# Joined borders with the squares from three sums, 18 idle products at the start, and a new order of the expert weights

## The chip, the cores and the metric

The kernel runs on one core of a Trainium2 chip. The metric is the device time of one execution in microseconds (us). The core's engines are TensorE (PE in the rows; PEld is its loading of weights), VectorE (DVE), ScalarE (ACT), GpSimd (POOL) and SyncE (SP), whose queue issues nearly all the transfers (DMA). Each engine runs its own queue in order; waits between the engines go by semaphores.

## The reference

Two layers of a decoder trunk on 256 tokens of width 1024. Each sub-layer normalises x, scales and shifts it by values made from c (adaLN), computes a token mixer or a channel mixer, and adds the normalised result times a gate:

```python
for layer in range(DEPTH):
    mod = (c_act @ w_ada[layer] + b_ada[layer])[:, None, :]
    shift_m, scale_m, gate_m, shift_f, scale_f, gate_f = jnp.split(mod, 6, axis=-1)
    h = rms_norm(x, g_pre_mix[layer]) * (1.0 + scale_m) + shift_m
    m = hybrid_mixer(h, w_in[layer], w_out[layer], ...)
    x = x + gate_m * rms_norm(m, g_post_mix[layer])
    h = rms_norm(x, g_pre_ffn[layer]) * (1.0 + scale_f) + shift_f
    if layer % 2 == 0:
        f = swiglu(h, ffn_w_gate[i], ffn_w_up[i], ffn_w_down[i])
    else:
        f = moe_swiglu(h, moe_w_router[i], moe_b_router[i], moe_w_gate[i], moe_w_up[i], moe_w_down[i])
    x = x + gate_f * rms_norm(f, g_post_ffn[layer])
```

The mixer joins 8 stick-breaking heads and 8 sparse heads. The channel mixer of layer 0 is one SwiGLU of width 2816; that of layer 1 sends each token to 2 of 8 experts, each a SwiGLU of width 3584. All is float32.

## The kernel before

**Stages.** Layer 0's mixer, layer 0's dense channel mixer (`ffn`), layer 1's mixer, the router, then the experts one after the other (`moe`). Tokens lie in two tiles t of 128. From 587 us to 1423 us of the span the experts run.

**Weights.** All weights come in units of 1 MB (`U`, 128x2048 float32). Units are loaded into a ring of six buffers named `raw` (`load`, L165 to L168), in `moe` also into tiles named `unit` (whole units with the tag a8, L994; half units with the tags g, y, f, t4, L1002). SP's queue issues these loads in the order of the program, and each waits there until its buffer is free. A place in the `moe` stage's memory is free when the mixer's tiles that lay there have been read for the last time. The list `plan` in `stream` says into which buffers the first 18 units of the experts go; later units take `raw`, t4 and a8 in turn (`ring`).

**Products.** A product in float32 is taken apart: ACT rounds a half unit to `whi` (L180), DVE (for the first units after a border GpSimd, by `lead`) subtracts it into `wlo` (L181), and PE makes three products (`mm3`, L196 to L198). An expert with few tokens ("short") is multiplied in plain float32 instead, with the weights as the moving side (L1054). An expert has 42 units: of each of its 7 chunks two for `moe_gate`, two for `moe_up`, two for `moe_down`, where a chunk's `moe_down` stands in the stream behind the next chunk's gate. The second gate unit of the second expert is therefore the 42nd of the stream.

**Borders.** Between layer 0's mixer and `ffn` (border 1) and between `ffn` and layer 1's mixer (border 2) stands, for each tile: `update` (L400: the squares of the result m by ACT, mg = m times the gate row by DVE, x += mg * r by DVE), `measure` (L240: the squares of the new x by ACT), `rows` (L248: xn = x * r' by DVE, L256), and `norm_parts` (L296): 8 transposes `xnT` on PE (L308), scale and shift `hf` by DVE and ACT in turn (L312, L314), `hh` by ACT (L316), `hlo` by DVE (L317). The first product of the next stage needs both. In border 1 m is itself a sum of two projected halves (L545), which starts when the sum of squares `sss` (L774) is there.

**Router.** `scorer` (L851) transposes the raw x (`xT`) and makes the logits with 8 columns; `route` (L880) picks experts and places; `gather` (L1152) brings the tokens of the first expert together by products with a 0/1 matrix.

**Start.** `first` (L330) transposes the normalised x (8 products `xnT`, L267) and waits for scale and shift of the first projection, which come from the adaLN weights; `pb` is the product for the bias table.

**Order.** The rows of each engine's queue stand in the order in which the program calls them, moved only where `behind` asks for one instruction to follow another.

## Time and profile before

| | us |
|---|---|
| time, median of 3 runs (lowest, highest) | 1440.67 (1439.38, 1440.95) |
| the profiled execution | 1441.2 |
| its span | 1439.4 |
| PE busy, share of the span | 1366.9, 95% |
| DVE busy | 984.6, 68% |
| ACT busy | 769.4, 53% |
| POOL busy | 16.6, 1% |

The mean clock that TensorE was granted is 0.971 of full speed. The span is cut by stage in the windows of the rows below, and read as follows: a stage in which PE is always busy is bound by PE; where PE sits idle, the timeline names what ended the idle time; a stage in which the DMA moves its top rate all along has transfers as its limit or close to it.

### The profile page before, as it was taken

How to read it: one execution, taken by the hardware profiler on the slowest of the kernel's cores; microseconds unless marked ns; L12 is line 12 of the kernel's file. 1: busy time of each engine (PE TensorE's matmuls, PEld its weight loads, DVE VectorE, ACT ScalarE, POOL GpSimd, SP SyncE). 2: the span in 40 equal slices, each digit the busy share in tenths (PEclk: the TensorE clock that was granted, in tenths of full speed). 3: DMA queues.
4: the chain of work that ended last, by engine and by line, in shares of the span. 5: the costliest groups of instructions: out<-in, count | busy, mean ns of one | idle time of the engine just before them, and what ended most of it. 6: DMA issues, size and time to landing. Idle time of an engine off the chain costs nothing.

```text
span 1439.4 us, 20261 instructions
## 1 busy us (share of the span) xinstructions
PE 1366.9 (95%) x7408; PEld 974.5 (68%) x7408; DVE 984.6 (68%) x1578; ACT 769.4 (53%) x1179; POOL 16.6 (1%) x24
## 2 busy tenths in 40 slices
PE   5899969999979999999999999999999999999996
PEld 5767659999877687534787434887435888788432
DVE  7677988877565785424998425997416989999413
ACT  3463654444554556223777324786325877787322
POOL 0100010000100000000000000000000000000000
PEclk9989979999989999899999999999999999999998
DMA  9935929888435285999999999999999999999994
GB/s 370 341 130 189 342 94 350 322 318 331 161 123 203 91 319 176 393 400 426 426 426 426 400 413 426 426 426 426 396 425 426 427 425 378 338 371 372 375 426 179
DMA packets 73479, 482.52 MB, mean 335 GB/s; under 512 B 10315, under 2 KB 10484, under 8 KB 18588
## 3 DMA queue, kind: packets, MB, share of 16 engines
q1 hardware_dynamic: 72876, 479.91, 83.5%
q0 software_dynamic: 496, 1.25, 0.4%
q8 instruction: 60, 0.98, 0.3%
q14 instruction: 47, 0.39, 0.1%
HBM read 479.87 MB, written 1.25 MB: 334 GB/s over the span
## 4 chain that ended last, share of the span: by engine, by line
PE 65%; DVE 3%; ACT 1%; issue 1%; DVEq 0%; ACTq 0%
PE moe_gate L1054 7%; PE moe_up L1054 7%; PE yacc L1054 7%; PE moe_gate L197 4%; PE moe_gate L196 4%; PE moe_gate L198 4%; PE yacc L197 4%; PE yacc L198 3%; PE yacc L196 3%; PE moe_up L197 3%; PE moe_up L198 3%; PE moe_up L196 3%; PE gT L1112 2%; PE gather L1190 1%; PE po L628 1%; DVE wlo L181 1%
## 5 line engine op out<-in xcount | busy, mean ns | idle before, releaser
L180 ACT ACTIVATE whi<-raw 128x1024 fp32r<-128x1024 f32 x260 | 271.7, 1058 | 156.4 <-PE ffn_gate L197 30.2
L181 DVE TENSOR_TENSOR wlo<-raw,whi 128x1024 fp32r<-128x1024 f32 x256 | 306.9, 1222 | 69.5 <-ACT whi L180 62.2
L181 DVE TENSOR_TENSOR wlo<-unit,whi 128x1024 fp32r<-128x1024 f32 x202 | 236.6, 1220 | 9.6 <-ACT whi L180 5.4
L180 ACT ACTIVATE whi<-unit 128x1024 fp32r<-128x1024 f32 x202 | 208.3, 1057 | 34.0 <-PE moe_up L198 17.0
L208 DVE CUSTOM_DVE_ANT_0 raw<-raw,cb,sm 128x1024 f32<-128x1024 f32 x96 | 120.5, 1278 | 1.0 <-DMA raw<-in_w_ada_dram 1.0
L1102 DVE TENSOR_TENSOR sg<-moe_gate,sg 64x512 f32<-64x512 f32 x28 | 19.1, 681 | 113.4 <-ACT sg L1101 113.4
L197 PE MATMUL moe_up<-wlo,xgh 128*128 128x512 f32 x224 | 88.5, 395 | 3.9 <-DVE wlo L181 3.9
L197 PE MATMUL yacc<-wlo,g 128*128 128x512 f32 x224 | 89.5, 400 | 0.3 <-DVE wlo L181 0.3
L196 PE MATMUL moe_gate<-whi,xgh 128*128 128x512 f32 x224 | 88.3, 394 | 0.0
L197 PE MATMUL moe_gate<-wlo,xgh 128*128 128x512 f32 x224 | 87.9, 392 | 0.0
L196 PE MATMUL moe_up<-whi,xgh 128*128 128x512 f32 x224 | 87.8, 392 | 0.0
L196 PE MATMUL yacc<-whi,g 128*128 128x512 f32 x224 | 87.8, 392 | 0.0
L198 PE MATMUL yacc<-whi,g 128*128 128x512 f32 x224 | 87.5, 391 | 0.0
L198 PE MATMUL moe_gate<-whi,xgl 128*128 128x512 f32 x224 | 87.4, 390 | 0.0
L198 PE MATMUL moe_up<-whi,xgl 128*128 128x512 f32 x224 | 87.4, 390 | 0.0
L1102 DVE TENSOR_TENSOR up<-moe_up,up 64x512 f32<-64x512 f32 x28 | 19.1, 683 | 72.7 <-ACT up L1101 72.7
L1054 PE MATMUL moe_up<-unit,xf 128*64 128x512 f32 x288 | 66.3, 596 | 0.0
L1054 PE MATMUL yacc<-unit,gf 128*64 128x512 f32 x272 | 62.2, 593 | 0.0
L1054 PE MATMUL moe_gate<-unit,xf 128*64 128x512 f32 x240 | 57.1, 598 | 0.0
L1101 ACT ACTIVATE sg<-moe_gate 64x512 f32<-64x512 f32 x28 | 16.6, 594 | 72.6 <-PE moe_gate L1054 72.5
L197 PEld LDWEIGHTS moe_up<-wlo,xgh 128*128 128x128 f32 x224 | 42.1, 188 | 16.5 <-DVE wlo L181 8.2
L196 PE MATMUL ffn_gate<-hh,whi 128*128 128x256 f32 x176 | 50.5, 287 | 2.5 <-ACT hh L316 2.4
(415 smaller groups left out, 2900.2 us busy)
## 6 DMA issues: line engine op xcount, KB each, us to landing
unit<-in_moe_gate_dram SPq DMA_DIRECT2D x66, 1024.0 KB, 12.9
unit<-in_moe_up_dram SPq DMA_DIRECT2D x56, 1024.0 KB, 12.5
unit<-in_moe_down_dram SPq DMA_DIRECT2D x54, 1024.0 KB, 14.6
raw<-in_w_ada_dram SPq DMA_DIRECT2D x48, 1024.0 KB, 6.8
raw<-in_moe_gate_dram SPq DMA_DIRECT2D x46, 1024.0 KB, 13.5
raw<-in_moe_down_dram SPq DMA_DIRECT2D x45, 1024.0 KB, 14.0
raw<-in_moe_up_dram SPq DMA_DIRECT2D x44, 1024.0 KB, 13.3
raw<-in_w_in_dram SPq DMA_DIRECT2D x16, 1024.0 KB, 6.2
```

Of the source, the lines that this page charges most:

```text
L180: self.last_hi = nc.scalar.activation(hi, w, AF.Copy)
L181: last_lo = (nc.gpsimd if self.count < 2 else nc.vector).tensor_sub(lo, w, hi.bitcast(F32))
L196: nc.tensor.matmul(out, lhsT=ahi, rhs=bhi, start=first, stop=False, skip_group_check=True)
L197: nc.tensor.matmul(out, lhsT=ahi, rhs=blo, start=False, stop=False, skip_group_check=True)
L198: nc.tensor.matmul(out, lhsT=alo, rhs=bhi, start=False, stop=last, skip_group_check=True)
L208: self.nc.vector.tensor_tensor_reduce(w[:, j], w[:, j], self.cb, 1.0, self.sm[:, b:b + 1], OP.mult, OP.add, self.modc[:, l, o:o + 1])
L628: nc.tensor.matmul(po[64 * g:64 * g + 64, :], lhsT=lhs, rhs=rhs, start=first[g], stop=last, skip_group_check=True)
L1054: m = nc.tensor.matmul(out[64 * kk:64 * kk + 64], lhsT=x[:, k], rhs=w[:, 512 * kk:512 * kk + 512], start=first and h == 0, stop=last and h ...
L1101: nc.scalar.activation(to, p[64:128], AF.Copy)
L1102: nc.vector.tensor_add(to, p[0:64], to)
L1112: nc.tensor.transpose(tr[0][:, j, 0:n], sg[0:n, P * j:P * j + P], self.ident[0:n, 0:n])
L1190: nc.tensor.matmul(p[:, a], lhsT=self.x[:, t, P * k:P * k + P], rhs=both[:, t], start=a == 0 and t == 0, stop=t == 1, skip_group_check=True)
```

## The change

**Borders.** `update`, `rows` and the transposes at both borders go. `ahead` prepares, before the result m is there: a row `ssr` of scale and gain laid over all partitions (8 more transposes on PE, named `rows`), `xsr` = x * ssr for both tiles (4 operations on 512 columns), the old sum of squares `sum0`, ssr times the gate row (2 operations), and the shift as `shT` (one transpose). `join` takes the squares of the new x from three sums: of x*x (known), of mg*x (`tensor_tensor_reduce`, 2 per tile), and of mg*mg (ACT). xs = m*ssr*gate*r + xsr is formed on DVE; the transposition is a product of xs with a diagonal matrix `dg` of r' (16 float32 products), added in PSUM to a product that lays down the shift (4 products of 512 columns, which need only `shT`). `hh` and `hlo` are taken from PSUM directly.

**Weights at the borders.** `foretell` loads and converts the first unit of the next stage before the border; GpSimd converts nothing any more. The conversions of `w_gates` wait for the border's last instructions.

**Idle products.** Products in bfloat16 on a matrix of ones, 512 columns wide, whose result nobody reads: 18 at the start between `xnT` and `pb`, 6, 4 and 7 in the scorer, 2 in the router.

**Router.** The logits have the weights as the stationary side (four groups of 32 columns, added up by one more product). The gather of a short expert has 128 columns where it had 64.

**Expert stream.** The new `plan` begins with whole units in the places a7 and a3, then the six `raw`, then the others. Every load follows the one before it from the first unit on.

```diff
-                            self.ffn(l, Phase(ph, t4=3, t2=3, h8=2))
+                            self.ffn(l, Phase(ph, t4=4, t2=4, h8=3))
...
-                self.moe(L - 1, Phase(ph, t4=2, t2=3, x4=2, f=2, y=2, g=2, a8=8))
+                self.moe(L - 1, Phase(ph, t4=2, t2=3, x4=2, f=2, y=2, g=2, **{f"a{i}": 1 for i in range(8)}))
...
+        if self.fore:
+            parts, self.fore = self.fore, None
+            yield from parts
+            return
...
-            with self.behind(*(self.chain if 2 <= self.count < 4 else self.lead if self.count < 2 else ())):
+            with self.behind(*(self.chain if self.count < 2 else ())):
                 self.last_hi = nc.scalar.activation(hi, w, AF.Copy)
-                last_lo = (nc.gpsimd if self.count < 2 else nc.vector).tensor_sub(lo, w, hi.bitcast(F32))
...
+    def foretell(self, src):
...
+        nc, parts, after = self.nc, [], self.conv
+        raw = self.load(src)
+        for h in range(2):
+            w = raw[:, h * (U // 2):(h + 1) * (U // 2)]
+            hi, lo = (self.mix.tile([P, U // 2], F32R, name=n, bufs=2) for n in ("fhi", "flo"))
+            with self.behind(*after):
+                nc.scalar.activation(hi, w, AF.Copy)
+                nc.vector.tensor_sub(lo, w, hi.bitcast(F32))
+            parts.append((h, *(p.rearrange("p (k f) -> p k f", k=4) for p in (hi, lo))))
+        return parts
...
+    def ahead(self, ph, l, gain, scale_i, shift_i, gm):
...
+        row = self.mix.tile([P, D], F32, name="ssr")
+        self.rows_of(self.affine(l, gain, scale_i), row)
+        p = self.bank("t", "shT")
+        nc.tensor.transpose(p[0:KT, 0:P], self.mod(l, shift_i), self.ident)
+        self.shT = self.mix.tile([KT, P], F32, name="shT")
+        nc.scalar.activation(self.shT, p[0:KT, 0:P], AF.Copy)
+        self.xsr = ph.tile([P, 2 * D + LINE], F32, name="xsr", tag="h8")[:, 0:2 * D].rearrange("p (t c) -> p t c", t=2)
+        self.sum0 = self.small.tile([P, 2], F32, name="sum0")
+        for t in range(2):
+            q = self.xsq[t]
+            nc.vector.tensor_add(self.sum0[:, t:t + 1], q[:, 0:1], q[:, 1:2])
+            for i in range(2):
+                cs = slice(512 * i, 512 * i + 512)
+                nc.vector.tensor_mul(self.xsr[:, t, cs], self.x[:, t, cs], row[:, cs])
+        for i in range(2):
+            cs = slice(512 * i, 512 * i + 512)
+            nc.vector.tensor_mul(row[:, cs], row[:, cs], gm[:, cs])
+        self.both_rows, self.pieces = (gm, row), []
+
+    def join(self, ph, t, src):
...
+        nc = self.nc
+        gm, gms = self.both_rows
+        ssq = self.small.tile([P, 2], F32, name="ssu")
+        sj = self.small.tile([P, 8], F32, name="sj")
+        mg = ph.tile([P, D], F32, name="mg", tag="t4")
+        mgs = src(None)
+        if mgs is None:
+            mgs = ph.tile([P, D], F32, name="mgs", tag="t4")
+        half = [slice(0, 512), slice(512, 1024)]
+        for i, cs in enumerate(half):
+            piece = src(i)
+            scr = self.small.tile([P, 512], BF16, name="scr")
+            nc.scalar.activation(scr, piece, AF.Square, accum_out=ssq[:, i:i + 1])
+            nc.vector.tensor_mul(mg[:, cs], piece, gm[:, cs])
+            scr = self.small.tile([P, 512], BF16, name="scr")
+            nc.scalar.activation(scr, mg[:, cs], AF.Square, accum_out=sj[:, i:i + 1])
+            junk = ph.tile([P, 512], F32, name="junk", tag="t2")
+            nc.vector.tensor_tensor_reduce(junk, mg[:, cs], self.x[:, t, cs], 2.0, sj[:, 2:3] if i else 0.0, OP.mult, OP.add,
+                                           sj[:, 2 + i:3 + i])
+            nc.vector.tensor_mul(mgs[:, cs], piece, gms[:, cs])
+        r = self.rstd(ssq[:, 1:2], D, "ru", base=ssq[:, 0:1])
+        nc.vector.tensor_add(sj[:, 4:5], sj[:, 0:1], sj[:, 1:2])
+        nc.vector.scalar_tensor_tensor(sj[:, 5:6], sj[:, 4:5], r, sj[:, 3:4], op0=OP.mult, op1=OP.add)
+        nc.vector.scalar_tensor_tensor(sj[:, 6:7], sj[:, 5:6], r, self.sum0[:, t:t + 1], op0=OP.mult, op1=OP.add)
+        nc.vector.tensor_scalar(sj[:, 7:8], sj[:, 6:7], 0.0, None, op0=OP.max)
+        r2 = self.rstd(sj[:, 7:8], D, "rn")
+        for i, cs in enumerate(half):
+            nc.vector.scalar_tensor_tensor(mgs[:, cs], mgs[:, cs], r, self.xsr[:, t, cs], op0=OP.mult, op1=OP.add)
+        dg = ph.tile([P, P], F32, name="dg", tag="t2")
+        scaled = nc.vector.tensor_scalar(dg, self.ident, r2, None, op0=OP.mult).ins
+        self.pieces.append((mgs, dg))
+        for cs in half:
+            with self.behind(*([scaled] if t else [])):
+                nc.vector.scalar_tensor_tensor(self.x[:, t, cs], mg[:, cs], r, self.x[:, t, cs], op0=OP.mult, op1=OP.add)
+        if t == 0:
+            return
+        self.hT = [[self.bank(b, "hT").rearrange("p (k t) -> p k t", k=4) for h in range(2)] for b in "sp"]
+        for out, (xs, dg) in zip(self.hT, self.pieces):
+            for h, p in enumerate(out):
+                nc.tensor.matmul(p, lhsT=self.shT, rhs=self.ident[0:KT, 4 * h:4 * h + 4, None].to_broadcast([KT, 4, P]),
+                                 start=True, stop=False, skip_group_check=True)
+            for h, p in enumerate(out):
+                for i in range(4):
+                    k = 4 * h + i
+                    nc.tensor.matmul(p[:, i], lhsT=xs[:, P * k:P * k + P], rhs=dg, start=False, stop=True, skip_group_check=True)
...
             if q == 0:
+                self.idle(18, self.last_turn, banks[5].rearrange("p m t -> p (m t)"))
...
             r = self.rstd(sq, 512, "ro")
...
+            if l == 0 and j == 0:
+                self.fore = self.foretell(self.ins["ffn_gate"][0])
...
             if l == 0:
-                self.update(ph, t, piece, gm, nc.vector)
+                self.join(ph, t, piece)
...
+        if l == 0:
+            self.ahead(ph, 0, G_PRE_FFN, 4, 3, gm)
...
+                self.fore = self.foretell(self.ins["w_in"][11 - 6])
...
+            if u == 7:
+                self.ahead(ph, 1, G_PRE_MIX, 1, 0, gm)
...
-            self.update(ph, t, lambda n: None if n is None else acc[t][n], gm, nc.vector)
+            self.join(ph, t, lambda n: None if n is None else acc[t][n])
...
+    def idle(self, n, after, warm=None):
...
+        warm = self.bank("p", "warm") if warm is None else warm
+        with self.behind(after):
+            for i in range(n):
+                self.nc.tensor.matmul(warm.rearrange("p (a t) -> p a t", a=4), lhsT=self.one,
+                                      rhs=self.one[:, None].to_broadcast([P, 4, P]), start=True, stop=True)
...
+        ws = ph.tile([P, KT, 32], F32, name="ws", tag="t2")
+        nc.gpsimd.memset(ws, 0.0)
...
+            if t:
+                self.total(after)
...
+                if h:
+                    self.idle(6 - 2 * t, last.ins)
...
-                    k = 4 * h + i
-                    nc.tensor.matmul(pl[:, 0:E], lhsT=xT[:, i], rhs=ws[:, k], start=k == 0, stop=k == KT - 1)
+                    nc.tensor.matmul(pl[32 * i:32 * i + 32, 0:P], lhsT=ws[:, 4 * h + i], rhs=xT[:, i], start=h == 0, stop=h == 1,
...
+                return nc.tensor.matmul(pl[:, 2 * P:2 * P + E], lhsT=part, rhs=self.sel[:, 0:E], start=True, stop=True,
...
+                self.idle(7, total(after).ins)
...
+        self.idle(2, last.ins)
...
-            plan = [None, None, None, "g", None, None, None, "y", "f", "t4", "a8", "a8", "a8", "a8", "a8", "a8", "a8", "a8"]
-            ring = [t for t in plan if t in (None, "t4", "a8")]
+            plan = ["a7", "a3", None, None, None, None, None, None, "g", "y", "a2", "a4", "a1", "a5", "a0", "a6", "f", "t4"]
+            ring = [t for t in plan if t not in ("g", "y", "f")]
...
-        ahead = [next(fetch) for i in range(4)]
+        made["g"] = tiles("g")
...
-        ahead += [next(fetch) for i in range(14)]
-        made.clear()
+        for i in range(8):
+            made[f"a{i}"] = ph.tile([P, U], F32, name="unit", tag=f"a{i}")
+        ahead = [next(fetch) for i in range(18)]
```

SP's queue, from the last load of layer 1's mixer (`in_w_out_dram`) to the experts' first loads. `raw` is the ring of six, `unit` a tile in the memory of `moe`. Before:

```order
L168 DMA raw<-in_w_out_dram 128x2048 [waits DVE_49]
L168 DMA raw<-in_moe_gate_dram 128x2048 [waits DMAHW5_49,DVE_49]
L168 DMA raw<-in_moe_gate_dram 128x2048 [waits DVE_49]
L168 DMA raw<-in_moe_up_dram 128x2048 [waits DMAHW6_49,DVE_49]
L168 DMA raw<-in_moe_gate_dram 128x2048 [waits DMAHW7_49,DVE_49]
L168 DMA raw<-in_moe_gate_dram 128x2048 [waits DMAHW0_49,DVE_49]
L168 DMA raw<-in_moe_up_dram 128x2048 [waits DMAHW1_49,DVE_49]
L1002 DMA unit<-in_moe_up_dram 128x1024 [waits PE_49]
```

After:

```order
L168 DMA raw<-in_w_out_dram 128x2048 [waits DVE_49]
L1112 DMA unit<-in_moe_gate_dram 128x2048 [waits DVE_49,PE_49,Activation_49]
L1112 DMA unit<-in_moe_gate_dram 128x2048 [waits DVE_49,PE_49,Pool_49]
L168 DMA raw<-in_moe_up_dram 128x2048 [waits DMAHW5_49]
L168 DMA raw<-in_moe_up_dram 128x2048
L168 DMA raw<-in_moe_gate_dram 128x2048 [waits DMAHW6_49]
L168 DMA raw<-in_moe_gate_dram 128x2048 [waits DMAHW7_49]
L168 DMA raw<-in_moe_up_dram 128x2048 [waits DMAHW0_49]
```

Two loads into the memory of `moe` now stand ahead of the six into `raw`. The waits of the first (a7) are for tiles of layer 1's mixer, on DVE for the second tile's last addition to x; those of the second (a3) are for `ws`, which lay there and is read last by the last product of the logits, and for the copy `xT`.

DVE's queue at border 1, from `sss` on. Before, up to the first tile's addition to x:

```order
L774 COPY sss<-ssb 128x2
L293 SCALAR_TENSOR_TENSOR ss<-modc,sm 128x8
L227 TENSOR_SCALAR rov<-sss,halfeps 128x2
L231 SCALAR_TENSOR_TENSOR rov<-ror,rov 128x1 x2
L232 SCALAR_TENSOR_TENSOR ror<-rov,ror 128x2
L545 SCALAR_TENSOR_TENSOR m<-wo,ror,m 128x512
L412 TENSOR_TENSOR m<-m,gm 128x512
...
L418 SCALAR_TENSOR_TENSOR x<-m,rur,x 128x512 x2
```

After, up to the same tile's three sums (`junk,sj` is the sum of mg*x):

```order
L863 COPY sss<-ssb 128x2
L331 TENSOR_TENSOR xsr<-x,ssr 128x512 x4
L334 TENSOR_TENSOR ssr<-ssr,gm 128x512 x2
L244 TENSOR_SCALAR rov<-sss,halfeps 128x2
L199 TENSOR_TENSOR flo<-raw,fhi 128x1024
L248 SCALAR_TENSOR_TENSOR rov<-ror,rov 128x1 x2
L249 SCALAR_TENSOR_TENSOR ror<-rov,ror 128x2
L632 SCALAR_TENSOR_TENSOR m<-wo,ror,m 128x512 x2
L354 TENSOR_TENSOR mg<-m,gm 128x512 x2
L358 ISA junk,sj<-mg,x 128x512
L358 ISA sj 128x1
L360 TENSOR_TENSOR m<-m,ssr 128x512
```

Between `sss` and the first sum for m stand seven more large operations (four `xsr`, two `ssr`, one `flo`); each half of m is then read by three DVE operations (L354, L358, L360) where one (L412) read it.

## Rows read from the trace of the kernel before

**Rows 1.** The page: TensorE's and the other engines' busy time over the whole span, and the shares of the chain of work that ended last.

```profile
PE 1366.9 (95%) x7408; PEld 974.5 (68%) x7408; DVE 984.6 (68%) x1578; ACT 769.4 (53%) x1179; POOL 16.6 (1%) x24
...
PE 65%; DVE 3%; ACT 1%; issue 1%; DVEq 0%; ACTq 0%
```

**Rows 2.** Windows of the expert stage: stretch in us, its length, busy time of PE, PEld, DVE, ACT and POOL, the granted clock as a share of full speed, the DMA share, GB/s.

```profile
575.00:640.00 65.00, 62.31 (x295) 29.84 (x297) 25.38 (x90) 18.19 (x36) 0.00 (x0) 0.89 0.94 389
640.00:700.00 60.00, 58.37 (x266) 30.62 (x263) 31.81 (x35) 27.93 (x37) 0.00 (x0) 1.00 1.01 426
...
820.00:880.00 60.00, 60.00 (x285) 22.23 (x284) 18.75 (x35) 19.41 (x34) 0.00 (x0) 1.00 0.99 407
```

**Rows 3.** Timeline of SP's queue between 518 and 600 us (start, time taken to issue, what, count), and last, of the experts' gate weights in 515 to 700 us, the time from issue to landing (minimum, median, maximum).

```profile
524.29 2.67 SPq L168 DMA_DIRECT2D raw<-in_moe_gate_dram  x2
...
548.03 0.33 SPq L168 DMA_DIRECT2D raw<-in_moe_up_dram  x1
555.19 1.91 SPq L1002 DMA_DIRECT2D unit<-in_moe_up_dram  x4
576.90 0.80 SPq L994 DMA_DIRECT2D unit<-in_moe_gate_dram  x2
...
DMA to landing us min/median/max: 4.8/13.6/19.9
```

**Rows 4.** The first expert: the timeline's first row of its products on PE, then two rows of the chain of waits (start, length; the gate products of two chunks that follow each other), and the timeline's row of ACT with the conversion of the second expert's first two units.

```profile
586.89 3.45 PE L1054 MATMUL moe_gate<-raw,xf 128*64 128x512 f32 x10
...
646.96 3.58 PE moe_gate L1054 x16
...
657.79 3.58 PE moe_gate L1054 x16
...
665.36 3.89 ACT L180 ACTIVATE whi<-unit 128x1024 fp32r<-128x1024 f32 x4
```

**Rows 5.** Timeline of PE at border 1 (in brackets the idle time before, and what ended it).

```profile
189.26 0.39 PE L198 MATMUL wo<-whi,os 128*128 128x512 f32 x1
198.44 4.02 PE L308 MATMUL xnT<-ident,xn 128*128 128x128 f32 x16 [8.79 <-DVE xn L256]
204.82 0.58 PE L196 MATMUL ffn_gate<-hh,whi 128*128 128x256 f32 x1 [2.36 <-ACT hh L316]
```

**Rows 6.** Timeline of DVE at border 1, and in the last row of POOL.

```profile
180.30 0.16 DVE L774 COPY sss<-ssb 128x2 f32<-128x2 f32 x1 [0.35 <-PE ssb L772]
...
187.03 2.06 DVE L231 SCALAR_TENSOR_TENSOR ruv<-rur,ruv 128x1 f32<-128x1 f32 x1 [0.55 <-ACT rur L228]
189.13 2.27 DVE L232 SCALAR_TENSOR_TENSOR rur<-ruv,rur 128x1 f32<-128x1 f32 x1
191.44 1.42 DVE L418 SCALAR_TENSOR_TENSOR x<-m,rur,x 128x512 f32<-128x512 f32 x2
192.77 0.75 DVE L545 SCALAR_TENSOR_TENSOR m<-wo,ror,m 128x512 f32<-128x512 f32 x1
...
199.95 0.88 DVE L256 TENSOR_SCALAR xn<-x,rnr 128x512 f32<-128x512 f32 x2
...
186.66 4.72 POOL L181 TENSOR_TENSOR wlo<-raw,whi 128x1024 fp32r<-128x1024 f32 x2 [142.10 <-ACT whi L180]
```

**Rows 7.** Prices of operations elsewhere: the gather of a later expert (timeline of PE; 16 float32 products of 128 columns, each in two rows), 8 transposes at the start (timeline of PE), and the page's group of DVE's conversions (busy, mean ns of one).

```profile
1161.44 3.73 PE L1152 MATMUL gather<-pmr,x 128*128 128x128 f32 x32
...
10.64 1.99 PE L267 MATMUL xnT<-ident,xn 128*128 128x128 f32 x8
...
L181 DVE TENSOR_TENSOR wlo<-raw,whi 128x1024 fp32r<-128x1024 f32 x256 | 306.9, 1222 | 69.5 <-ACT whi L180 62.2
```

**Rows 8.** Border 2: timeline of PE, and of DVE the first row that reads the finished result of tile 0.

```profile
392.94 0.39 PE L198 MATMUL acc<-whi,gl 128*128 128x512 f32 x1
399.43 3.99 PE L308 MATMUL xnT<-ident,xn 128*128 128x128 f32 x16 [6.10 <-DVE xn L256]
406.12 0.58 PE L196 MATMUL pc<-hh,whi 128*128 128x256 f32 x1 [2.71 <-ACT hh L316]
...
387.06 0.69 DVE L412 TENSOR_TENSOR mg<-acc,gm 128x512 f32<-128x512 f32 x1 [2.03 <-ACT scr L411]
```

**Rows 9.** Windows at half clock: columns as in rows 2.

```profile
193.20:210.20 17.00, 9.13 (x38) 8.04 (x39) 15.38 (x41) 11.88 (x30) 0.00 (x0) 0.50 0.13 54
398.00:411.60 13.60, 9.36 (x40) 8.28 (x41) 11.48 (x28) 9.41 (x21) 0.00 (x0) 0.50 0.20 69
572.10:589.10 17.00, 14.31 (x66) 12.60 (x66) 7.91 (x42) 3.42 (x11) 0.00 (x0) 0.50 0.81 324
15.70:22.50 6.80, 4.39 (x16) 3.11 (x17) 5.71 (x9) 3.93 (x5) 0.00 (x0) 0.50 1.03 430
```

**Rows 10.** Router: timeline of PE with the logits of tile 0 and of tile 1, and of DVE with the last addition to x.

```profile
570.06 1.95 PE L875 MATMUL logits<-ws,xT 128*128 128x8 f32 x16 [1.77 <-ACT xT L869]
...
573.45 3.42 PE L875 MATMUL logits<-ws,xT 128*128 128x8 f32 x16
...
570.36 1.41 DVE L418 SCALAR_TENSOR_TENSOR x<-m,rur,x 128x512 f32<-128x512 f32 x2
```

**Rows 11.** Start: timeline of PE, the first product after the transposes, and a later wait of the same projection.

```profile
18.11 1.45 PE L150 MATMUL pb<-oh,tab 33*8 33x384 f32 x2 [5.48 <-DVE hf L276]
...
40.96 0.39 PE L196 MATMUL first<-hh,whi 128*128 128x256 f32 x1 [1.81 <-ACT whi L180]
```

More of the change, by code (lines that the diff above doesn't have):

```diff
@@ L987, in stream @@
                 if tag is None:
-                    yield self.load(src, after=last if i >= len(plan) else ())
-                    if i > len(plan):
-                        last = self.loaded,
-                elif tag == "a8":
-                    unit = ph.tile([P, U], F32, name="unit", tag=tag)
-                    with self.behind(*(last if i >= len(plan) else ())):
+                    unit = self.load(src, after=last)
+                    last = self.loaded,
+                    yield unit
+                elif tag[0] == "a":
+                    unit = made.pop(tag, None) or ph.tile([P, U], F32, name="unit", tag=tag)
+                    with self.behind(*last):
                         self.loaded = nc.sync.dma_start(unit, src).ins
@@ L999, in stream @@
                     unit = tiles(tag)
-                    with self.behind(*(last if i >= len(plan) else ())):
+                    with self.behind(*last):
                         for h, t in enumerate(unit):
```

70 lines of the change are left out of this document (37 added, 33 removed).

## The prediction

> **What bounds the kernel now.** I read the page first: PE is busy 95% of the span and makes up 65% of the chain that ended last [rows 1]. So a gain can only come out of some 60 us of PE's idle time, out of PE's time at half clock, or out of PE work left out; and a loss comes whenever PE is made to wait. Then I went by stage. In the windows of the experts the transfers run at 426 GB/s as their top rate while PE is hardly idle [rows 2]: two limits lie side by side there, and which one ends last depends on how many units lie in store. The timeline of PE and ACT shows why. A short expert takes a chunk of six units in 657.79 - 646.96 = 10.83 us [rows 4]; at 426 GB/s six units of 1,048,576 bytes land in 6 x 2.46 = 14.8 us. The first expert is short, and so lives on its store. SP's queue shows where that comes from: the first units are issued at 524.29, and eight units (six into `raw`, two as four halves) by 557 [rows 3], while the first expert product starts at 586.89 [rows 4]. Last I read the borders: there PE waits 8.79 us for xn and 2.36 us for hh [rows 5], 6.10 and 2.71 us at border 2 [rows 8], and the granted clock is at its lower level (1.2 of 2.4 GHz, "half" below) in both and around the router [rows 9].
>
> **The change part by part.**
>
> *Expert stream.* In the new queue the two first loads, a7 and a3, wait for the end of layer 1's mixer: a7 for the second tile's last addition to x (570.36 + 1.41 = 571.8 in the trace), a3 for the last product of the logits (573.45 + 3.42 = 576.9) [rows 10]. The six loads into `raw`, whose buffers come free from 524 to 548 [rows 3], stand behind them in SP's queue, and an engine's queue runs in order. So nothing but a7 is issued before tI, the end of the logits. I put tI at 575.9: the logits of tile 1 take 3.42 us at half clock where those of tile 0 take 1.95 [rows 10], the idle products may win up to 1.5 of that, and I take 1. From there the sum is by transfers alone: the second unit of the stream lands 4.8 us after its issue (the shortest time in the trace [rows 3]), each later one 2.46 us behind it, so the 42nd lands at 575.9 + 4.8 + 40 x 2.46 = 679.1. That is the second expert's second gate unit, which ACT starts to convert at 665.36 + 3.89 / 2 = 667.3 [rows 4]. PE and ACT arrive there no later than before (the borders move both sides alike), so the stall is **+11.8 us**. Bounds: at 430 GB/s (the last of [rows 9]) and tI 0.5 earlier still 10.4; at 389 GB/s, the rate of 575 to 640 us in which the ring had waits of its own [rows 2], 2.70 us a unit and 21.2. I take the value at 426, because from 640 us on the queue is never without a free buffer and shows that rate. For later short experts I add nothing: around 820 to 880 us the rate is 407 [rows 2], so 60 x (1 - 407/426) = 2.7 us of transfer time were unused there, and a long expert in between rebuilds some store; up to 6 us is kept for the range.
> The Trainium skill, page "Perfetto Trace Analysis", section Roofline, gives 358 GB/s as a core's share of the memory and some 435 as the ceiling of its 16 DMA engines when it works alone. By 358 a unit would take 2.93 us and the stall would be about 30 us; the trace's 426 lies well above that and just under the other figure, so the sum stays with the trace.
>
> *Border 1.* What counts is the time from `sss` to the first `ffn_gate` product: 204.82 - 180.30 = 24.5 us now [rows 5, 6]. Of it 20.5 are DVE's, up to the last xn (199.95 + 0.88), and 4.0 lie behind. Two tiny DVE operations took 2.06 and 2.27 us in this stretch, just while POOL's two conversions ran (186.66, 4.72 us) [rows 6]; without POOL's work they should take some 0.2 each, so about 4 us of the 20.5 go. Against that DVE now has 28 operations of 512 columns between `sss` and the second `dg`: xsr 4, ssr 2, m 4, mg 4, sums 4, m*ssr 4, xs 4, the first tile's x 2. Two such follow each other in 192.77 - 191.44 = 1.33, 0.67 each [rows 6]: 18.8 us. The sum operation `tensor_tensor_reduce` has no row; I give it the same price as other operations with two inputs of that size, with the range below. One `flo` adds 1.2 [rows 7], some 26 tiny operations about 2.6 (0.16 for `sss` [rows 6], less their overlap), one return from ACT 0.5: 23.1, so +2.6. Behind `dg` come 8 products: 16 like them take 3.73 us in a gather at full clock [rows 7], so 1.9, or 3.7 at half; then hh and hlo: from the last transpose to the first product it is 2.36 now [rows 5], and since the first hh now waits for the last of these products, I put 2.7. That is 4.6 to 6.4 against 4.0; the stretch is at half clock now [rows 9] and PE waits no less, so +1.9. The 9 added transposes cost PE 9 x 1.99 / 8 = 2.2 [rows 7] in a stretch where it is busy; some fall in waits, +1.5. Sum **+6.0**; bounds +2 (full clock behind `dg`, transposes hidden, tiny operations at half price) and +9 (0.75 for each large one [rows 6], all at half clock, nothing hidden).
>
> *Border 2.* Here `xsr` and `ssr` are made long before. DVE starts on tile 0 at 387.06 [rows 8]; 18 large operations (12.1), 24 tiny (2.4) and a return (0.5) bring the second `dg` to 402.1, then 4.6 to 6.4 as above: 406.7 to 408.5 against 406.12 [rows 8]. I take +1.5, and +1 for 9 transposes: **+2.5**, bounds 0 and +4.
>
> *First unit ahead, GpSimd off.* `foretell` moves two conversions on ACT and DVE ahead of each border; the one on DVE that falls between `sss` and `dg` is counted above, the others lie beside PE's work. The conversions taken from GpSimd return to DVE behind the border, where one unit is ready ahead: nothing.
>
> *Start.* 18 idle products stand in the 5.48 us before `pb` [rows 11]. Their price has no row. At the least (a transpose's 0.25 [rows 7]) they take 4.5 us and fit; as long as a logits product at half clock (0.43) they take 7.7 and delay `pb` by some 2 us. If they keep the clock up, the window at half clock (4.39 us of PE work in it [rows 9]) gives back at most 2.2. Either way the same projection waits 1.81 us for ACT at 39 us [rows 11], which swallows most of it. **0**, bounds -1.5 and +2.
>
> *Router.* At half clock 14.31 us of PE work lie around it [rows 9], so up to 7 us could be won, but behind the router PE now waits for the stream; only tI counts, above. **0**.
>
> **Sum.** 11.8 + 6.0 + 2.5 = +20.3 us on the profiled execution of 1441.2. The median of the runs is 0.5 lower, so 1440.7 + 20.3 = **1461 us**. The bounds together give +11 to +42, mostly far less than all upper ends at once.
>
> **Rivals.**
> 1. *Faster: the borders' chain is short.* If DVE keeps pace with the projection (each half of m handled while PE still makes the next), only the last half's steps are left behind PE's last product: four large operations, a dozen tiny, a return and 4.6 us, about 9, against 15.2 (204.82 - 189.65) and 12.8 now [rows 5, 8], so -6 and -4. For it: POOL's conversions and eight `hf` go. Against it: the six operations and `flo` put before m in an in-order queue. It ends as faster only if the stream's stall is under 7 us, so if tI comes 5 us earlier than I think; with a stall of nothing, 1430. The point that decides: the second `dg` no later than 2 us after the last `wo` product, and the first expert loads before 571.
> 2. *The stall repeats or the clock falls.* (a) The store is not rebuilt, and the next short experts wait as well, 6 us in each of three: 1479. (b) In the first expert PE works 1.81 of each 2.46 us; if the clock fell to half in half of this stretch, a unit would take (1.81 + 3.61) / 2 = 2.71 instead of 2.46, over 28 units 7 us: 1468. For it: with PE busy 65% and less, the stretches of rows 9 are at half clock. Against it: each wait is under a microsecond.
> The Trainium skill, page "TensorE: Matmul & The Clock Gate", section on oscillation of the clock, describes kernels whose products are shorter than the wait for each tile's transfer and whose clock falls anew at each tile; it speaks for (b), and no stretch of this trace with a wait for each unit shows it.
> 3. *The stream is not held.* The waits of a7 and a3 end with the attention, as the first unit's does now at 555.19 [rows 3]; then the store is only some units short, nothing stalls, and the borders alone are left: 1449. Against it: `ws` is read until the last logits product.
> 4. *Between.* The borders gain 5 to 8 and the stream costs as much: about 1441.
>
> **How the numbers follow.** Forecast 0.60, rival 2 0.17, rival 3 0.08, rival 4 0.05, rival 1 0.10. A measurement of this kernel can tell about 0.2%, 3 us, from no change. Faster 0.10, within 0.05, slower 0.85. The range leaves out rivals 1 and 4 below and the worst of rival 2 above: 1444 to 1480.
>
> **What would show it.** In the profile after: SP's first expert load at about 572 and the second at about 576, the six `raw` right behind; PE waiting in the first expert for DMA, in sum about 12 us, at a transfer rate of 426; the product after border 1 some 30 us behind `sss`, with DVE busy all that time; no 2 us operation on DVE there; the window of the start hardly moved. The prediction is wrong if expert loads are issued before 560, if PE never waits for a unit in the first expert, or if `dg` stands less than 20 us behind `sss`.

## The result and the profile after

| | before | after |
|---|---|---|
| time, median of 4 runs (lowest, highest), us | 1440.81 (1439.38, 1441.89) | 1457.10 (1455.12, 1458.59) |
| ratio, 95% interval | | 1.0113 [1.0095, 1.0130] |
| profiled execution: time, span | 1441.2, 1439.4 | 1455.1, 1453.3 |

The changed kernel is 16.3 us slower, 1461 was forecast; the profiled execution is the fastest of its four, 13.9 above that of before. Where PE is at the same point of the program, by the two timelines:

| PE's first or last product of | before | after | later by |
|---|---|---|---|
| `ffn_gate`, behind border 1 | 204.82 | 210.98 | 6.2 |
| the projection `pc`, behind border 2 | 406.12 | 413.88 | 7.8 |
| the logits (end) | 576.9 | 579.5 | 2.6 |
| the first expert | 586.89 | 586.18 | -0.7 |
| the second expert | 668.57 | 683.99 | 15.4 |
| span | 1439.4 | 1453.3 | 13.9 |

So the loss at the borders (7.8) is given back by the time the experts start, and the first expert alone then costs 16.1.

The page after (busy time; chain that ended last), against [rows 1]:

```profile
PE 1384.1 (95%) x7515; PEld 976.2 (67%) x7515; DVE 999.2 (69%) x1620; ACT 769.5 (53%) x1177; POOL 7.0 (0%) x21
...
PE 62%; DMA 7%; DVE 4%; ACT 2%; issue 1%; SPq 0%; DVEq 0%; ACTq 0%
```

PE's share of busy time is the same, and tells nothing: PE does 17 us more (idle products and others). What is new is DMA with 7% of the chain, where it had none. SP's queue from 515 us on, against [rows 3], and in the second fence what SP waited for between 560 and 600 us (us in total, times, longest):

```profile
523.75 1.53 SPq L168 DMA_DIRECT2D raw<-in_w_out_dram  x2
575.97 3.14 SPq L1112 DMA_DIRECT2D unit<-in_moe_gate_dram  x2
579.16 0.90 SPq L168 DMA_DIRECT2D raw<-in_moe_up_dram  x2
```

```profile
SPq L1112 <- DVE x L502: 50.6, 1, 50.6
...
SPq L1112 <- PE logits L979: 2.4, 1, 2.4
```

Between the last load of the mixer and the first of the experts SP issues nothing for 50 us. It stands before a7 until DVE's last addition to x, then before a3 until the last logits product. In the kernel before, eight units had been issued by 557 us and ten by 570 [rows 3].

The windows, against [rows 2]; then PE in the first expert, a stretch of the timeline, and its first two products for the second expert; then, from the chain of waits, the transfer that ends last (start, length, what), and ACT's next conversions:

```profile
640.00:700.00 60.00, 48.24 (x200) 17.73 (x199) 14.96 (x19) 15.26 (x22) 0.00 (x0) 0.97 1.02 421
...
820.00:880.00 60.00, 60.00 (x288) 23.50 (x288) 17.68 (x35) 16.64 (x32) 0.00 (x0) 1.00 1.01 421
```

```profile
655.52 1.94 PE L1173 MATMUL moe_gate<-unit,xf 128*64 128x512 f32 x8 [0.55 <-DMA unit<-in_moe_gate_dram]
658.01 1.94 PE L1173 MATMUL moe_up<-unit,xf 128*64 128x512 f32 x8 [0.55 <-DMA unit<-in_moe_up_dram]
...
683.99 0.50 PE L213 MATMUL moe_gate<-whi,xgh 128*128 128x512 f32 x1 [1.24 <-ACT whi L184]
685.24 0.67 PE L214 MATMUL moe_gate<-wlo,xgh 128*128 128x512 f32 x1 [0.76 <-DVE wlo L185]
```

```profile
663.24 19.62 DMA raw<-in_moe_gate_dram
...
682.88 2.01 ACT L184 ACTIVATE whi<-raw 128x1024 fp32r<-128x1024 f32 x2 [4.85 <-DMA raw<-in_moe_gate_dram]
685.36 2.00 ACT L184 ACTIVATE whi<-unit 128x1024 fp32r<-128x1024 f32 x2 [0.48 <-DMA unit<-in_moe_gate_dram]
```

In this stretch PE gets a unit every 658.01 - 655.52 = 2.49 us, waits 0.55 for each and works 1.94. The last link before the second expert is the transfer of its first gate unit (in `raw`), the 41st of the stream, landed at 663.24 + 19.62 = 682.86; the 42nd (in `unit`) is there at 685.3, when ACT starts on it. By the formula of the prediction, with the measured end of the logits, the 42nd would land at 579.5 + 4.8 + 40 x 2.46 = 682.7, and so 2.6 earlier than it did: the 40 units took 2.53 us each on average, because the transfers ran at 404 GB/s from 579 to 600 us and at 419 to 421 behind. Around 820 us PE is not kept waiting, and the unused rate of 407 is now used (421).

Border 1 on PE, against [rows 5], and on DVE, against [rows 6]:

```profile
201.07 3.50 PE L385 MATMUL hT<-dg,m 128*128 128x128 f32 x16 [2.68 <-DVE dg L370]
206.23 2.05 PE L385 MATMUL hT<-dg,m 128*128 128x128 f32 x16 [1.67 <-DVE dg L370]
210.98 0.55 PE L213 MATMUL ffn_gate<-hh,fhi 128*128 128x256 f32 x1 [2.70 <-DVE hlo L395]
```

```profile
179.84 1.23 DVE L199 TENSOR_TENSOR flo<-raw,fhi 128x1024 fp32r<-128x1024 f32 x1 [0.92 <-ACT fhi L198]
180.99 0.42 DVE L854 TENSOR_TENSOR sqsum<-sqsum,sqs 128x256 f32<-128x256 f32 x1
...
182.47 0.16 DVE L863 COPY sss<-ssb 128x2 f32<-128x2 f32 x1 [0.67 <-PE ssb L861]
182.54 2.49 DVE L331 TENSOR_TENSOR xsr<-x,ssr 128x512 f32<-128x512 f32 x4
184.95 1.28 DVE L334 TENSOR_TENSOR ssr<-ssr,gm 128x512 f32<-128x512 f32 x2
...
186.29 1.22 DVE L199 TENSOR_TENSOR flo<-raw,fhi 128x1024 fp32r<-128x1024 f32 x1
...
205.89 0.28 DVE L370 TENSOR_SCALAR dg<-ident,rnr 128x128 f32<-128x128 f32 x1
```

From `sss` to the end of the second `dg` 23.7 us (23.1 were forecast), from there to the first product 4.8, in all 28.5 against 24.5. PE's two waits for `dg` are short (2.68, 1.67) because `shT` products and the first tile's products lie between; what counts is the sum.

Border 2 on PE, against [rows 8]:

```profile
400.58 3.70 PE L380 MATMUL hT<-ident,shT 8*128 8x512 f32 x8
404.21 2.63 PE L385 MATMUL hT<-dg,mgs 128*128 128x128 f32 x16
410.40 3.78 PE L385 MATMUL hT<-dg,mgs 128*128 128x128 f32 x16 [3.55 <-DVE dg L370]
413.88 0.58 PE L213 MATMUL pc<-hh,fhi 128*128 128x256 f32 x1
```

The windows of the clock, against [rows 9] (columns as there), and the start, against [rows 11]:

```profile
12.00:20.00 8.00, 6.32 (x27) 2.95 (x26) 6.91 (x14) 2.81 (x4) 0.00 (x0) 0.99 1.00 414
193.90:204.10 10.20, 7.17 (x18) 4.03 (x19) 10.03 (x34) 3.77 (x12) 0.00 (x0) 0.50 0.00 1
405.60:415.70 10.10, 6.55 (x30) 6.25 (x30) 7.78 (x23) 4.05 (x10) 0.31 (x1) 0.50 0.08 10
572.00:586.00 14.00, 12.00 (x101) 7.63 (x100) 10.28 (x45) 5.91 (x19) 0.00 (x0) 1.00 0.64 242
```

```profile
12.92 4.09 PE L948 MATMUL first<-one 128*128 128x512 bf16 x18
18.38 0.81 PE L150 MATMUL pb<-oh,tab 33*8 33x384 f32 x2 [1.38 <-DVE hf L294]
```

The router runs at full clock now, where 17 us were at half. 18 idle products take 4.1 us, fit ahead of `pb`, and `pb` starts 0.27 later than before.

### The profile page after: what moved, and what is told of

Its sections match the earlier page's. It is cut to its first block, busy times and chain, and to the rows that moved or that the text cites. A ratio compares the mean times of both kernels' runs of the same rounds, so it can differ in the third digit from the quotient of the medians.

```text
span 1453.3 us, 20504 instructions
## 1 busy us (share of the span) xinstructions
PE 1384.1 (95%) x7515; PEld 976.2 (67%) x7515; DVE 999.2 (69%) x1620; ACT 769.5 (53%) x1177; POOL 7.0 (0%) x21
## 4 chain that ended last, share of the span: by engine, by line
PE 62%; DMA 7%; DVE 4%; ACT 2%; issue 1%; SPq 0%; DVEq 0%; ACTq 0%
PE yacc L1173 5%; PE moe_gate L1173 5%; PE moe_up L1173 5%; PE moe_gate L214 4%; PE moe_gate L215 4%; PE moe_gate L213 4%; PE yacc L213 3%; PE yacc L214 3%; PE yacc L215 3%; PE moe_up L214 3%; PE moe_up L215 3%; PE moe_up L213 3%; DMA raw<-in_moe_gate_dram 3%; PE gT L1231 1%; DMA unit<-in_moe_up_dram 1%; DMA unit<-in_moe_gate_dram 1%
## 5 line engine op out<-in xcount | busy, mean ns | idle before, releaser
L184 ACT ACTIVATE whi<-raw 128x1024 fp32r<-128x1024 f32 x256 | 266.8, 1057 | 152.3 <-PE ffn_up L214 29.9
L1173 PE MATMUL yacc<-unit,gf 128*64 128x512 f32 x296 | 68.1, 595 | 3.8 <-DMA unit<-in_moe_down_dram 3.0
L1173 PE MATMUL moe_gate<-unit,xf 128*64 128x512 f32 x264 | 64.4, 599 | 0.9 <-DMA unit<-in_moe_gate_dram 0.7
L1173 PE MATMUL moe_up<-unit,xf 128*64 128x512 f32 x256 | 59.2, 597 | 1.1 <-DMA unit<-in_moe_up_dram 1.1
L1220 ACT ACTIVATE sg<-moe_gate 64x512 f32<-64x512 f32 x28 | 16.6, 595 | 72.3 <-PE moe_gate L1173 72.3
L1173 PEld LDWEIGHTS yacc<-unit,gf 128*64 128x64 f32 x296 | 20.4, 137 | 47.3 <-issue 39.2
```

Source lines behind the costliest of these rows:

```text
L184: self.last_hi = nc.scalar.activation(hi, w, AF.Copy)
L1173: m = nc.tensor.matmul(out[64 * kk:64 * kk + 64], lhsT=x[:, k], rhs=w[:, 512 * kk:512 * kk + 512], start=first and h == 0, stop=last and h ...
L1220: nc.scalar.activation(to, p[64:128], AF.Copy)
```

## The experiments

The theory after the result: the loads of the experts are held in SP's queue by a7 and a3, and the first expert, which takes its units faster than they can land, pays for it; the borders cost time of their own. Rivals: the borders and the added work on PE are the whole loss, and the waits in the first expert only fill time that the router would have won; or the joined borders are a gain, hidden by the stream. Times are medians of 4 to 12 executions; "before" ran beside each of them on the same chip and had 1441.4 to 1441.9. The changed kernel did not, so that a difference to its 1457.1 is uncertain by some 1 us ("before" had 1440.8 in that measurement). old_cold, old_nofore and join_b2 ran on another chip than the rest.

**1. Three or all units of `raw` first** (two kernels, raw3 and raw6gy; the second has the places g and y ahead as well).

```diff
-            plan = ["a7", "a3", None, None, None, None, None, None, "g", "y", "a2", "a4", "a1", "a5", "a0", "a6", "f", "t4"]
+            plan = [None, None, None, "a7", "a3", None, None, None, "g", "y", "a2", "a4", "a1", "a5", "a0", "a6", "f", "t4"]
```

```diff
+            plan = [None, None, None, None, None, None, "g", "y", "a7", "a3", "a2", "a4", "a1", "a5", "a0", "a6", "f", "t4"]
```

> Changed kernel, but three of the six loads into raw stand ahead of a7 and a3 in the plan. Theory (the loads are held until the end of the logits, and the first expert then waits for transfers): three units less have to land after the logits, 3 x 2.49 = 7.5 us off the stall, 1457.1 - 7.5 = 1449.6, within 2. Rival (the borders and the added PE work cost the 16 us, the waits in the first expert only cover what the router would win): no change, 1457 within 2.

> Changed kernel, but the plan begins with the six raw and the places g and y, then a7, a3 and the rest. Theory: eight units are in flight before the logits end, the 42nd unit lands at about 579.5 + 4.8 + 32 x 2.49 = 664, before the second expert asks for it (some 666), so no wait for a transfer in the first expert and the whole stall of some 16 us goes: 1441 within 2. Rival (borders): 1457 within 2.

raw3: 1451.3. raw6gy: 1439.3, ratio to before 0.9975 [0.9961, 0.9989]. Three units ahead take 5.8 off (7.5 were expected), eight take 17.8. SP's queue of raw6gy, and all that PE waited for in 586 to 700 us:

```profile
530.87 2.67 SPq L168 DMA_DIRECT2D raw<-in_moe_gate_dram  x2
...
561.65 1.91 SPq L1120 DMA_DIRECT2D unit<-in_moe_up_dram  x4
578.38 3.10 SPq L1112 DMA_DIRECT2D unit<-in_moe_down_dram  x2
```

```profile
PE moe_up L214 <- DVE wlo L185: 1.0, 2, 0.6
PE scatter L1200 <- ACT whi L184: 0.5, 1, 0.5
```

No wait for a transfer is left. The stall is the order of the loads, and it shrinks with the number of units in store.

**2. Only the stream, in the kernel before** (before_plan).

```diff
-            plan = [None, None, None, "g", None, None, None, "y", "f", "t4", "a8", "a8", "a8", "a8", "a8", "a8", "a8", "a8"]
+            plan = ["a8", "a8", None, None, None, None, None, None, "g", "y", "a8", "a8", "a8", "a8", "a8", "a8", "f", "t4"]
...
-                    yield self.load(src, after=last if i >= len(plan) else ())
-                    if i > len(plan):
-                        last = self.loaded,
+                    unit = self.load(src, after=last)
+                    last = self.loaded,
+                    yield unit
...
-                    with self.behind(*(last if i >= len(plan) else ())):
+                    with self.behind(*last):
...
```

> The kernel before, with only the stream of the change: two units in the places with the tag a8 first, then six raw, then g and y and the rest, every load ordered behind the one before it. Theory (order of the loads alone makes the stall): the first load waits for the last logits product (576.9), the 42nd unit lands 4.8 + 41 x 2.48 = 106.5 later at 683.4, against 667.3: +16, so 1457 within 3. Rival (without the slower borders the stream catches up, or a lead of this size is not needed): 1441 to 1446.

1454.9, ratio 1.0092 [1.0073, 1.0112]: old borders, no idle products, and 13.2 slower. The first scatter product (in the second expert's stretch) comes 16.6 later than before (694.44 against 677.84), and 4 of that are given back by the end; the changed kernel gives back 4.1 in the same stretch, and raw6gy, in which nothing stalls, 3.6 (678.43 at that product, span 1436.4). So the new plan and its ring are worth some 4 us in the later experts; by what, is not taken apart here.

**3. The changed plan without ordering its loads** (after_nochain).

```diff
-                    unit = self.load(src, after=last)
+                    unit = self.load(src, after=last if i >= len(plan) else ())
...
-                    with self.behind(*last):
+                    with self.behind(*(last if i >= len(plan) else ())):
...
```

> The changed kernel with its own plan, but without ordering the first 18 loads one behind the other; built so, the six loads into raw stand ahead of a7 and a3 in SP's queue. Theory: as with the raw first, six units are in store: the 42nd lands at 579.5 + 4.8 + 34 x 2.49 = 669 against some 666, a stall of 3 left: 1444 within 2. Rival (the plan's places, not the ordering, hold the loads): 1457.

1441.9, where 1444 was expected. In the built program the six `raw` then stand first, whatever the plan says. What held them was that every load was asked to follow the one before it: the plan's order alone would not have done it. So a queue does not simply have the order of the calls, as was said of the kernel before: there too the six `raw` stand ahead of g, which its plan has fourth.

**4. Old borders in the changed kernel** (raw6gy_old, with the plan of raw6gy).

```diff
-                self.join(ph, t, piece)
+                self.update(ph, t, piece, gm, nc.vector)
...
-        hh, hl = self.norm_parts(ph, True)
+        hh, hl = self.norm_old(l, ph, G_PRE_FFN, 4, 3)
...
-            self.join(ph, t, lambda n: None if n is None else acc[t][n])
+            self.update(ph, t, lambda n: None if n is None else acc[t][n], gm, nc.vector)
```

(`norm_old` is `norm_parts` of the kernel before, and is used at border 2 as well; both calls of `ahead` go.)

> As raw6gy, with the old borders (update, rows, transposes, hf) at both places; the first unit is still converted ahead and GpSimd still converts nothing. Theory (the joined borders cost time: DVE's longer queue behind sss): border 1 some 5 us shorter, the 18 added transposes gone (1 to 2), against it a half clock window that is longer by 3.4 after border 2: 3 to 5 us faster than raw6gy, about 1437. Rival (the joined borders win on their own): slower than raw6gy by 3 or more.

1425.4, ratio 0.9876 [0.9857, 0.9896]: 13.9 faster than raw6gy, where 3 to 5 were expected. The sign was right, the size not. By the two traces the first product behind border 1 comes 11.1 earlier than in raw6gy, the one behind border 2 13.9: the whole difference lies at the borders. Its border 1 on PE and DVE:

```profile
194.08 4.02 PE L416 MATMUL xnT<-ident,xn 128*128 128x128 f32 x16 [4.88 <-DVE xn L273]
200.40 0.58 PE L213 MATMUL ffn_gate<-hh,fhi 128*128 128x256 f32 x1 [2.30 <-ACT hh L424]
```

```profile
181.23 0.16 DVE L886 COPY sss<-ssb 128x2 f32<-128x2 f32 x1 [0.74 <-PE ssb L884]
...
195.59 0.88 DVE L273 TENSOR_SCALAR xn<-x,rnr 128x512 f32<-128x512 f32 x2
```

From `sss` to the last xn it takes 15.2 us, in the kernel before 20.5 [rows 6], in the changed one (to `dg`) 23.7. I had set the joined border against the old one with GpSimd's conversions in it, and left the old one without them out of account.

**5. The early work ahead of `sss`** (raw6gy_early2): `gate_row` and `ahead` are called two steps of the attention earlier (the plan is that of raw6gy).

```diff
         next(pairs)
+        if l == 0:
+            gm = self.gate_row(l, ph, 2, G_POST_MIX)
+            self.ahead(ph, 0, G_PRE_FFN, 4, 3, gm)
         next(pairs)
         sss = next(pairs)
-        gm = self.gate_row(l, ph, 2, G_POST_MIX)
-        if l == 0:
-            self.ahead(ph, 0, G_PRE_FFN, 4, 3, gm)
+        if l:
+            gm = self.gate_row(l, ph, 2, G_POST_MIX)
```

> As raw6gy, with xsr, ssr and the first unit's conversion on DVE ahead of the last attention steps, so ahead of sss. Theory A (the place in the queue is what costs at border 1): the 4.9 us of these operations leave the time from sss to the first product, 1441 - 5 = 1436. Theory B (DVE is busy all along ahead of sss as well, so the amount of its work counts and not the place): sss comes later by nearly as much, 1440 to 1441.

1439.4, as raw6gy. On DVE:

```profile
177.78 2.50 DVE L331 TENSOR_TENSOR xsr<-x,ssr 128x512 f32<-128x512 f32 x4 [0.33 <-ACT ssr L482]
...
187.79 0.42 DVE L856 TENSOR_TENSOR sqsum<-sqsum,sqs 128x256 f32<-128x256 f32 x1 [4.04 <-ACT sqs L854]
...
188.92 0.16 DVE L865 COPY sss<-ssb 128x2 f32<-128x2 f32 x1 [0.27 <-PE ssb L863]
...
208.15 0.29 DVE L370 TENSOR_SCALAR dg<-ident,rnr 128x128 f32<-128x128 f32 x1
```

The stretch from `sss` to `dg` is 4.2 shorter than the 23.7, and `sss` comes later by more than that (188.92 against 181.25 in raw6gy). So the place wins nothing, as Theory B says, but its reason does not hold: DVE is not busy all along ahead of `sss`, it waits 4.04 us there for ACT's squares `sqs`. The early work now stands among the attention's own steps, which end later; what holds them up is not taken apart.

**6. GpSimd's conversions given to DVE in the kernel before** (before_vec).

```diff
-                last_lo = (nc.gpsimd if self.count < 2 else nc.vector).tensor_sub(lo, w, hi.bitcast(F32))
+                last_lo = nc.vector.tensor_sub(lo, w, hi.bitcast(F32))
```

> The kernel before, with GpSimd's conversions at both borders (four in all) given to DVE, nothing else. Theory (DVE's two operations of 2.06 and 2.27 us, and the first addition to x at border 2, are drawn out by GpSimd's conversions beside them): 4.0 us go at border 1 and some 2 at border 2, and two conversions of 1.15 come into DVE's queue at each: about -2, 1439. Rival (they wait for something else): the conversions only add, +2 to +4.

1440.8, ratio 0.9989 [0.9980, 0.9999], barely clear of no change; -2 was expected. The tiny operations take 0.2 again, but the conversions now stand among them in DVE's queue, so only about 1 of the 4 us stays:

```profile
188.02 1.23 DVE L181 TENSOR_TENSOR wlo<-raw,whi 128x1024 fp32r<-128x1024 f32 x1
189.16 0.21 DVE L231 SCALAR_TENSOR_TENSOR ruv<-rur,ruv 128x1 f32<-128x1 f32 x1
189.40 1.22 DVE L181 TENSOR_TENSOR wlo<-raw,whi 128x1024 fp32r<-128x1024 f32 x1
190.54 0.15 DVE L232 SCALAR_TENSOR_TENSOR rur<-ruv,rur 128x1 f32<-128x1 f32 x1
```

**7. Without the first unit ahead** (old_nofore), **without the idle products of the router** (old_cold), **without the 18 at the start** (old_no18), all from raw6gy_old.

```diff
-            if l == 0 and j == 0:
-                self.fore = self.foretell(self.ins["ffn_gate"][0])
...
-                self.fore = self.foretell(self.ins["w_in"][11 - 6])
```

```diff
-                if h:
-                    self.idle(6 - 2 * t, last.ins)
...
-                self.idle(7, total(after).ins)
+                total(after)
...
-        self.idle(2, last.ins)
```

```diff
-                self.idle(18, self.last_turn, banks[5].rearrange("p m t -> p (m t)"))
```

> As raw6gy_old, without the conversion of the first unit ahead of the two borders; DVE then converts it behind the border. Theory (the first unit converted ahead is what turns GpSimd's absence into a gain): at each border ACT and DVE convert before the first product can be finished, 2 to 3 us each: about 1430. Rival (only GpSimd's absence counts): 1425 to 1426.

> As raw6gy_old, without the 6, 4, 7 and 2 idle products in the scorer and the router. Theory (with the stream out of the way they keep the clock at full level from the logits to the first expert product: 11.9 us there with them, 16.8 in the kernel before at half clock): 3 to 5 us slower than raw6gy_old, about 1429.5. Rival (the clock there is bought with as much time on PE): within 1.

> As raw6gy_old (new stream with the six raw, g and y first; old borders), without the 18 idle products at the start. Theory (the projection at the start waits for ACT's conversions later on, which takes up what the clock gives): within 1.5 of raw6gy_old, 1425. Rival (the full clock at the start is a gain that stays): 2 to 4 us slower.

old_nofore: 1432.6, 7.2 slower than raw6gy_old (some 5 were expected). Its profiled execution took 1438.7, but lost the other 6 us elsewhere: from `sss` to the first product behind border 1 it is 4.1 longer than in raw6gy_old, and from there to the first behind border 2 3.4. Behind border 1 PE waits for ACT, which converts only after `hh`; DVE has a multiplication of adaLN ahead of its conversions:

```profile
208.11 0.58 PE L213 MATMUL ffn_gate<-hh,whi 128*128 128x256 f32 x1 [5.08 <-ACT whi L184]
```

old_cold: 1428.0, 2.5 slower (3 to 5 were expected). The gather of the first expert runs at half clock again and takes 2.6 longer; first old_cold, then raw6gy_old:

```profile
572.79 6.42 PE L1289 MATMUL gather<-pmr,x 128*128 128x128 f32 x32 [0.88 <-DVE pmr L1269]
```

```profile
571.70 3.84 PE L1292 MATMUL gather<-pmr,x 128*128 128x128 f32 x32 [0.34 <-DVE pmr L1272]
```

old_no18: 1425.3, against 1425.4, so the 18 idle products bring nothing that four executions can tell. The traces can't price them: the profiled execution is the slowest of the four (1429.8), because at 57 us PE waited 6.80 for the conversion of weights that landed late, and old_nofore, which has the idle products, waits 5.20 at the same place; raw6gy_old waits 0.21 there.

**8. One border old, one joined** (join_b2): raw6gy_old with `ahead`, `join` and `norm_parts` at border 2 alone.

```diff
-            self.update(ph, t, lambda n: None if n is None else acc[t][n], gm, nc.vector)
+            self.join(ph, t, lambda n: None if n is None else acc[t][n])
...
-            hh, hl = self.norm_old(l, ph, G_PRE_MIX, 1, 0)
+            hh, hl = self.norm_parts(ph, False)
```

> As raw6gy_old at border 1, joined border as in raw6gy at border 2. By the traces of the two, border 2 takes 13.2 us joined and 10.4 old, plus nine transposes: 2.9 + 1 to 2, so 1425.4 + 4 = 1429.5, and border 1 has the other 10. Rival (the two borders are not independent: the time of one hides in the other's wait): 1425 or 1435 and more.

1430.3. Of the joined borders' 13.9 us, border 2 has 4.9 and border 1 the other 9.0. By the traces of raw6gy and raw6gy_old it is 2.8 and 11.1, so the split is known to some 2 us only.

## Why the prediction was right

*The total.* On the profiled execution +20.3 was forecast and +13.9 came (+16.3 in the medians, since the profiled execution is the fastest of its four). At the end of the logits the forecast has PE 8.5 - 1.0 = 7.5 later, the table 2.6; from there to the second expert both add 12.8. The other 1.5 were won in the later experts. So the mechanism was right, and most of the error is gains ahead of the experts that the sum did not have.

*Expert stream, +11.8.* The mechanism is shown: SP's row of 50.6 us, the waits of PE for each unit, the doses of experiments 1 and 3, and experiment 2, which has the stream alone. That its size came out is in part luck. The sum let the second expert wait for the 42nd unit, and its first product waits for the 41st, which is 2.5 less; and it took 2.46 a unit where the average was 2.53, which is 2.6 more over 40 units. Counted from the first expert's first product to the second's, the stretch is 16.1 longer (97.8 us against 81.7), not 11.8. I wrote that a gain in the router counts for nothing, because PE waits for the stream anyway. So it is, but the time from the last logits product to the first expert's fell from 10.0 to 6.7 us, and these 3.3 reappear as stall, as does the 1.0 by which the sum moved the end of the logits without moving PE's arrival: 11.8 - 2.5 + 2.6 + 3.3 + 1.0 = 16.2. Of the 97.8 us PE sits idle 12.3, as forecast; the other 3.8 lie in PE's busy time, since eight products that start anew take 1.94, where units of 16 followed each other every 3.43 to 3.49 us before.

The Trainium skill, page "Perfetto Trace Analysis", section Roofline, gives some 435 GB/s as a single core's ceiling and 358 as its share. The 421 of the window from 640 to 700 us lie just under the first and well above the second.

*Border 1, +6.0.* Measured 28.5 against 24.5 us from `sss`, and 2.2 by which `sss` is later (182.47 against 180.30, of which 0.8 came from the stages ahead): 6.2 in all. The parts differ more than the sum: up to `dg` 3.2 more instead of 2.6 (23.7 us where the forecast had 23.1), behind it 0.8 more instead of 1.9, because the second tile's products ran at full clock (2.05 us for 16). And `sss` is later not only by the transposes on PE: the first of the two conversions of `foretell`, which the sum put beside PE's work, stands on DVE ahead of `sqsum`, of which `sss` is made. The sum operation with no row took 0.68 to 0.74, as priced.

*Border 2, +2.5.* 1.6 later (7.8 - 6.2), within its bounds: 0.4 between the last `ffn` product and the first `pc` (13.2 against 12.8), 1.2 in the stretch ahead of it, where the transposes are.

*Start, 0.* 0.27 at `pb`, and experiment 7 shows no effect.

*What was not in the sum.* Layer 1's mixer gave back 3.4 us between its first product (406.12, 413.88) and the first of its output projection (525.12, 529.45). Before, 5.5 us of its first products lay at half clock, after 1.9, which is 1.8 us; of the rest, a wait of 0.8 is gone at 421. From the output projection to the end of the logits 1.7 were won, where the sum had 1.0. Behind the start of the second expert 2.6 were lost up to the first scatter product (see the clock below) and 4.1 gained from there on. The total was right in part because the range was wide (+3 to +39) and because errors of both signs met.

*Rivals.* The clock did not fall with each unit (rival 2b): it is full through the whole first expert, and falls once, behind the waits of 1.24 and 0.76 us with which the second expert begins:

```profile
586.20:684.00 97.80, 85.49 (x390) 28.65 (x387) 27.09 (x77) 24.26 (x45) 0.00 (x0) 1.00 1.01 419
...
685.40:688.80 3.40, 3.40 (x9) 2.64 (x10) 3.27 (x3) 2.35 (x3) 0.00 (x0) 0.50 1.01 422
```

The Trainium skill, page "TensorE: Matmul & The Clock Gate", section "HAM oscillation — how this bites in real kernels", describes a clock that falls anew at each tile when the wait for a tile's transfer outlasts the work on it. Here the work is the longer part (1.94 us against 0.55), and the trace shows no such fall in the first expert.

The one spell cost something all the same: its nine products start 0.43 us apart, 0.23 at full clock, and with the wait of 0.76 that makes the 2.6 us above. What the prediction said for this rival was misread: in the windows of [rows 9] PE is busy for 54 to 84% of the time, not for 65% and less. Rival 2a, a stall in the later short experts, fell too: behind 700 us PE waits for no transfer. Rival 3, a stream that is not held, fell with SP's wait of 50.6 us. Rival 1, the short chain at the borders, fell by experiments 4 and 8: the joined borders are 13.9 slower than the old ones once GpSimd is quiet and the first unit is ready. Rival 4, a gain at the borders as large as the stream's loss, fell with it.

The change thus holds a gain and two losses. The gain (first unit ahead, GpSimd off, full clock in the router, the new ring) is 16 us, as raw6gy_old shows against before; the joined borders cost 14, the order of the first loads 18. Of the gain the first unit ahead has 7.2, the router 2.5 and the new ring some 4 (by the traces); the rest is not taken apart. The version with the gain alone, raw6gy_old, beats both kernels.

## What to carry to other kernels

In a queue that runs in order, a load that must wait for memory delays every load behind it, so those whose buffers are free come first; and asking each load to follow the one before it takes from the scheduler the freedom to put that right. A chain made shorter on paper is to be counted in operations of the engine that is busy there: the joined border saves ACT's passes and adds DVE work, and DVE was the engine that PE waited for. A stage that lives on a store of prefetched data must be costed by the time of landing of the unit that the stage behind it waits for first. A gain between the release of its loads and its start turns into waiting (here 3.3 us in the router); a gain ahead of the release counts in full (here 3.4 in layer 1's mixer).

## What the runs showed that was not expected

Two DVE operations on one column each took 2.06 and 2.27 us beside GpSimd's conversions [rows 6], and about 0.2 when DVE did those itself; where the conversion was moved ahead of the border, that stretch shrank by 5.3 us (20.5 to 15.2), more than the 4.0 that stand in the two rows. What made up the rest is not taken apart.
